# One step of a two-layer diffusion backbone: modulation in units of 1024 columns, and the low one-hot rows by VectorE

## The chip, the core and the metric

The kernel runs on one core of a Trainium2 chip. The core has TensorE (PE), which multiplies matrices, VectorE (DVE), ScalarE (ACT), GpSimd (POOL) and SyncE (SP). SP issues nearly all DMA transfers, in the order of the program; POOL issues the indirect gathers. Work on one engine runs in program order, and the engines wait for each other by semaphores. The metric is the device time of one execution in microseconds.

## The reference

Two layers run over 384 tokens, 128 of a prompt and 256 of a sample. Cut to what matters here:

```python
def adaln(cond, w, b):
    m = jax.nn.silu(cond) @ w + b
    return jnp.split(m[..., None, :], 6, axis=-1)

def layer(x, l, cond, ctx):
    sh1, sc1, g1, sh2, sc2, g2 = adaln(cond, w_mod[l], b_mod[l])
    y, new_ctx = token_mixer(modulate(x, sh1, sc1), w_in[l], ...)
    x = layer_norm(DN_ALPHA * x + g1 * y, ln1_g[l], ln1_b[l])
    f = peer(modulate(x, sh2, sc2), peer_wq[l], peer_keys[l], peer_u[l], peer_v[l])
    x = layer_norm(DN_ALPHA * x + g2 * f, ln2_g[l], ln2_b[l])

def peer(h, wq, keys, u_tab, v_tab):
    s = jnp.einsum('thpd,hpkd->thpk', q, keys)      # q = t @ wq
    sv, si = lax.top_k(s, PEER_TOPK)
    ...                                             # 16 experts e, gates g for each of 8 heads
    act = jax.nn.gelu(jnp.einsum('td,ted->te', tb, u_tab[eb])) * gb
    return jnp.einsum('te,ted->td', act, v_tab[eb])
```

`cond` is one vector of 1024 for the prompt and one for the sample, and `w_mod[l]` is 1024 x 6144: each layer has six modulation vectors of 1024 (shift, scale, gate for the mixer and for the experts). `token_mixer` is one projection `h @ w_in`, a state-space scan, two attentions, three branch projections and `w_out`.

## The kernel before

**Weights and buffers.** Every large weight comes as a tile `w` of 128 x 1024 f32 (0.52 MB) from one pool of eight buffers (`N_RAW`): `w_in` blocks, `w_mod` tiles, `peer_wq` blocks, the chunks `peer_uT` and `peer_v`, and also the staging tiles of the gate table. A load is issued by SP (L210, L1148) when its buffer's last reader is done. A projection block is cast by ACT (L222, `uh`), its rest is taken by DVE or POOL (L224, `ul`), and PE runs 24 matmuls for it (L368 to L370).

**Modulation.** The work is 48 units (layer, vector, half of 512 columns by quarters). `adaln_unit` loads two tiles (`load_k`), runs eight matmuls of `condT` (L259, which the trace shows as sixteen records) over four column groups of the PE array, ACT copies the sums to `modp` (L261), and, when the next unit is begun or at a flush, two matmuls with a selection (L265) turn them into columns, to which ACT adds the bias into `mcol` (L268). The function `adaln(n, ...)` begins n units and finishes those begun earlier. It is called in five places: in layer 0's start, two units before every second `k`, each flushed, and then the ACT rows `hraw` (L444) that need them; in `blocks`, which hands out projection blocks, one unit after each second block until `N_FILL` (16 in layer 0, 8 in layer 1) are used; after the mixer's branches, `N_AD` (4 each, as far as there are units); and in `tick` in layer 0's retrieval, one unit a block from block 6 on.

**Experts.** `finding` (the retrieval) runs over 16 `wq` blocks: queries (L947), keys, transposes, and on DVE the top-16 search. The first 35 chunks of `u` (`LAG` - 1) are multiplied whole (`u_product`, L1164, sixteen records a chunk): 14 or 18 of them behind the retrieval, the others in the gate stage; each step first loads the chunk of the next step.

**Gate stage.** `gate_table` writes, for each of 256 sample tokens, a 128 x 128 table of gates to DRAM (`gd`), as a product of one-hot rows. In each of 16 batches of 16 tokens DVE makes `oa` (L997), `ol` (L999) and `ohh` = `ol` x `ghT` (L1001), all 128 x 2048 f16, in two buffers each; sixteen ACT instructions scale `ol` by `glT` in place (L1004); PE multiplies `oa` with `ohh` and `ol` (L1014, L1015), 32 matmuls; four ACT copies go to two `w` tiles (L1018), which SP writes to `gd` (L1021). `slot` hangs two gathers of `peer_u` rows (L1057) and their dot products on DVE (L1062) behind an instruction of the batch; the dot products of the prompt's tokens run in this way beside all that.

**Order.** Within a stage a scheduler orders the instructions of each engine by due times; `tc.issue_after` and `slot` pin some of them. The order of SP is the program's: a load that waits for a buffer holds back all that is queued behind it.

Of the kernel before, what the change touches and what calls it, by code (L numbers as in the profile page):

```python
# [155 lines left out]
def hybrid_step(ctx: ExitStack, tc: tile.TileContext, A, O):  # L156
# [71 lines left out]
    fill_ps, fill_n, first = [None], [0], [0]  # L228


    def cond_prep(sp, ps1):
# [12 lines left out]
        for l in range(DEPTH):
            bm = mk(sp, [48, 128], "bm", bufs=2)
            dma(out=bm, in_=A["b_mod"][l].rearrange("(k p) -> k p", p=128))
            ps = mk(ps1, [128, 512], "pt")
            T.transpose(ps[:, :48], bm, ident[:48, :48])
            V.tensor_copy(bmT[:, l], ps[:, :48])
            for part in (1, 4):  # L250
                V.tensor_scalar(bmT[:, l, part * KD:(part + 1) * KD], bmT[:, l, part * KD:(part + 1) * KD], 1.0, None, op0=ALU.add)
# [166 lines left out]
    def mixer(l, stack, right, ps1):  # L418
# [940 lines left out]
```

## Time and profile before

| | us |
|---|---|
| median of 3 runs (lowest, highest) | 2998.48 (2995.82, 3007.12) |
| the profiled execution | 3004.09 |
| its span in the trace | 3002.3 |
| PE busy | 2855.6 (95%) |
| DVE busy | 2309.1 (77%) |
| ACT busy | 1396.8 (47%) |
| POOL busy | 824.8 (27%) |

The stages follow one another: layer 0 has its mixer to about 560 us, retrieval to about 717, gate stage to about 862 and then the main loop over the 128 chunks; layer 1 the same from about 1540, with the retrieval from 2046, the gate stage from 2195 to 2326. Busy shares are means over stages with different limits, so a window or a chain is read for each. A chain names, for each stretch of time, the engine that was working or the transfer that was landing when everything behind it waited. A matmul on f32 data shows as two records. Engine time that others wait for is on the path; idle time of an engine that isn't on the path costs nothing.

### The profile page before, as it was taken

The numbers are of one execution on the slowest core, as the hardware profiler recorded it, in microseconds if no ns is written. First come the engines' busy times: TensorE is split into PE (matmuls) and PEld (weight loads), VectorE is DVE, ScalarE is ACT, GpSimd is POOL, SyncE is SP. The second block draws the span as 40 slices with busy tenths as digits, with TensorE's granted clock in tenths as the row PEclk, the third lists the DMA queues.
The fourth block names the chain that finished last, engine by engine and source line by source line (L and its number), as shares of the span: only waits on it lengthen the run. The fifth ranks groups of instructions, "written<-read, shape, count | busy, mean of one in ns | idle before, by whom it ended". The sixth has DMA issues, their size and how long they took to land.

```text
span 3002.3 us, 48719 instructions
## 1 busy us (share of the span) xinstructions
PE 2855.6 (95%) x17953; PEld 2479.3 (83%) x17953; DVE 2309.1 (77%) x4888; ACT 1396.8 (47%) x2861; POOL 824.8 (27%) x566
## 2 busy tenths in 40 slices
PE   7999999999889999999969999999987999999996
PEld 5888889877779999998858888898876999999985
DVE  3645654599669999998976466547986999999988
ACT  4544543225754444444445455432178544444443
POOL 1000000002334455554540000000033444555554
PEclk9999999999889999999979999999999999999998
DMA  6454322565999999999934432233569999999994
GB/s 246 151 159 146 95 72 87 182 223 167 316 364 408 391 392 396 393 391 369 379 97 144 127 93 74 85 111 113 156 217 371 418 395 392 394 391 394 393 364 166
DMA packets 299328, 767.09 MB, mean 256 GB/s; under 512 B 42770, under 2 KB 113874, under 8 KB 299090
## 3 DMA queue, kind: packets, MB, share of 16 engines
q1 hardware_dynamic: 225362, 495.51, 46.2%
q0 software_dynamic: 73728, 268.47, 23.5%
q8 instruction: 141, 2.31, 0.3%
q14 instruction: 97, 0.79, 0.1%
HBM read 726.92 MB, written 36.96 MB: 254 GB/s over the span
## 4 chain that ended last, share of the span: by engine, by line
PE 74%; DVE 11%; DMA 6%; ACT 4%; issue 4%; POOL 1%; SPq 0%; POOLq 0%; ACTq 0%; DVEq 0%
PE hp L1167 6%; PE out L1243 6%; PE hp L1169 6%; PE out L1245 6%; PE hp L1168 6%; PE out L1244 6%; PE pp L368 5%; PE pp L369 5%; PE pp L370 5%; PE hp L1164 4%; DMA w<-in_peer_uT 3%; PE pp L947 2%; ACT ol L1004 2%; DVE vl L224 2%; DVE tn L1073 2%
## 5 line engine op out<-in xcount | busy, mean ns | idle before, releaser
L1057 POOL DMA_INDIRECT prow<-in_peer_u,ei x256 | 363.1, 1418 | 763.1 <-DVE prow L1062 523.5
L1068 POOL DMA_INDIRECT prow<-in_peer_v,ei x256 | 382.4, 1494 | 350.1 <-DVE tn L1073 308.6
L222 ACT CAST vh<-w 128x1024 fp32r<-128x1024 f32 x256 | 268.9, 1050 | 367.9 <-issue 285.8
L1167 PE MATMUL hp<-hh,uh 128*128 128x256 f32 x1488 | 434.7, 292 | 0.0
L1169 PE MATMUL hp<-hh,ul 128*128 128x256 f32 x1488 | 417.1, 280 | 0.0
L1168 PE MATMUL hp<-hl,uh 128*128 128x256 f32 x1488 | 416.5, 280 | 0.0
L1245 PE MATMUL out<-vh,al 128*128 128x512 f32 x1024 | 400.0, 393 | 3.6 <-DVE al L1230 3.6
L1244 PE MATMUL out<-vl,ah 128*128 128x512 f32 x1024 | 397.5, 390 | 2.9 <-DVE vl L224 2.9
L1243 PE MATMUL out<-vh,ah 128*128 128x512 f32 x1024 | 392.9, 400 | 1.4 <-ACT ah L1228 1.4
L224 DVE TENSOR_TENSOR vl<-w,vh 128x1024 fp32r<-128x1024 f32 x256 | 315.8, 1234 | 62.7 <-ACT vh L222 44.0
L1073 DVE SCALAR_TENSOR_TENSOR tn<-prow,pact,tn 128x1024 f32<-128x1024 f32 x254 | 325.4, 1281 | 2.7
L1155 ACT CAST uh<-w 128x1024 fp32r<-128x1024 f32 x186 | 195.2, 1050 | 252.6 <-PE hp L1168 240.6
L368 PE MATMUL pp<-hh,uh 128*128 128x384 f32 (+1 forms) x848 | 297.9, 351 | 7.5 <-ACT hh L344 3.8
L1062 DVE SCALAR_TENSOR_TENSOR prow<-prow,tn 128x1024 f32<-128x1024 f32 x256 | 302.4, 1219 | 0.1
L1164 PE MATMUL hp<-hs,w 128*128 128x256 f32 x1120 | 270.1, 398 | 30.0 <-DMA w<-in_peer_uT 30.0
L370 PE MATMUL pp<-hh,ul 128*128 128x384 f32 (+1 forms) x848 | 297.0, 350 | 1.4 <-POOL ul L224 1.4
L369 PE MATMUL pp<-hl,uh 128*128 128x384 f32 (+1 forms) x848 | 294.8, 348 | 0.2 <-DVE xr L494 0.2
L1167 PEld LDWEIGHTS hp<-hh,uh 128*128 128x128 f32 x1488 | 281.1, 189 | 0.0
L1169 PEld LDWEIGHTS hp<-hh,ul 128*128 128x128 f32 x1488 | 281.1, 189 | 0.0
L1168 PEld LDWEIGHTS hp<-hl,uh 128*128 128x128 f32 x1488 | 281.1, 189 | 0.0
L224 DVE TENSOR_TENSOR ul<-w,uh 128x1024 fp32r<-128x1024 f32 x124 | 149.8, 1208 | 162.2 <-ACT uh L222 158.2
L1164 PEld LDWEIGHTS hp<-hs,w 128*128 128x128 f32 x1120 | 218.8, 200 | 63.4 <-DMA w<-in_peer_uT 33.1
(401 smaller groups left out, 5637.9 us busy)
## 6 DMA issues: line engine op xcount, KB each, us to landing
w<-in_peer_uT SPq DMA_DIRECT2D x256, 512.0 KB
w<-in_peer_v SPq DMA_DIRECT2D x256, 512.0 KB
w<-in_w_in SPq DMA_DIRECT2D x104, 512.0 KB
w<-in_w_mod SPq DMA_DIRECT2D x96, 512.0 KB
gd<-w SPq DMA_DIRECT2D x64, 512.0 KB
gt<-gd SPq DMA_DIRECT2D x64, 512.0 KB
w<-in_peer_wq SPq DMA_DIRECT2D x32, 512.0 KB
w<-in_w_branch SPq DMA_DIRECT2D x24, 512.0 KB
```

Of the source, the lines that this page charges most:

```text
L224: e.tensor_tensor(lo, src, hi.bitcast(F32), op=ALU.subtract)
L368: T.matmul(o, wh[:, k, :], hh[:, k, :], start=(k == 0), stop=False)
L369: T.matmul(o, wh[:, k, :], hl[:, k, :], start=False, stop=False)
L370: T.matmul(o, wl[:, k, :], hh[:, k, :], start=False, stop=(k == KD - 1))
L1073: V.scalar_tensor_tensor(acc, row, act[:, j:j + 1], acc, op0=ALU.mult, op1=ALU.add)
L1164: T.matmul(o, ut[0][:, k, :], hs[:, k, :], start=(k == 0), stop=(k == KD - 1))
L1167: T.matmul(o, uh[:, k, :], hh[:, k, :], start=(k == 0), stop=False)
L1168: T.matmul(o, uh[:, k, :], hl[:, k, :], start=False, stop=False)
L1169: T.matmul(o, ul[:, k, :], hh[:, k, :], start=False, stop=(k == KD - 1))
L1243: T.matmul(o, ah[:, ts], vh[:, ns], start=f, stop=False)
L1244: T.matmul(o, ah[:, ts], vl[:, ns], start=False, stop=False)
L1245: T.matmul(o, al[:, ts], vh[:, ns], start=False, stop=e)
```

## The change

**Modulation** is made in 12 units of 1024 columns instead of 48. `UNITS` lists them; the first two hold four k of shift and of scale of layer 0 each, the others one vector. A unit loads eight tiles (the host lays `w_mod` out that way), and each tile is used by four matmuls of 256 columns (32 in a unit, as many in all as before). ACT copies once, two transposes of 128 x 128 replace the selections, and two DVE additions (four in the first two units) take the bias and write `mcol`. The host also lays out `b_mod` and the conditions, so their transposes at the start go. At the start one unit runs before k = 0 and one before k = 4. `blocks` begins one after every sixth block (`FILL_BY`), five in layer 0 and at most two in layer 1, where one is left; one stands behind the branches of layer 0; `tick` begins one at blocks 9, 12 and 15 of layer 0's retrieval.

**The low one-hot rows** are made by one DVE instruction a batch, `ol` x `glT`, with `glT` now f16. `slot` hangs on it instead of on `ohh`.

**Chunks ahead of the main loop** are loaded three steps ahead (`U_AHEAD`), the first three before the retrieval loop.

```diff
-N_FILL = (16, 8)
-N_AD = (4, 4)
+N_FILL = (5, 2)
+FILL_BY = 6
+N_AD = (1, 1)
+U_AHEAD = 3
-R_AD = 4
+UNITS = [((0, 0, 0, 4), (0, 1, 0, 4)), ((0, 0, 4, 4), (0, 1, 4, 4))]
+UNITS += [((l, part, 0, 8),) for l, part in ((0, 2), (0, 3), (0, 4), (1, 0), (1, 1), (0, 5), (1, 2), (1, 3), (1, 4), (1, 5))]
...
-    def adaln_unit(l, part, hb, ps1, tags):
+    def adaln_unit(u, ps1, tags):
 
-        w = load_k(A["w_mod"][l, part * 4 + hb])
         ps = mk(ps1, [128, 512], tags[0])
         for k in range(KD):
-            q = k % 4
-            T.matmul(ps[32 * q:32 * q + 32, :256], condT[:, k, :], w[k], start=(k < 4), stop=(k >= 4), tile_position=(0, 32 * q))
+            w = mk(wst, [128, RAWC], "w")
+            dma(out=w, in_=A["w_mod"][u, k])
+            for q in range(4):
+                T.matmul(ps[32 * q:32 * q + 32, :256], condT[:, k, :], w[:, q * 256:(q + 1) * 256], start=(k == 0), stop=(k == KD - 1), tile_position=(0, 32 * q))
         mp = mk(outer, [128, 256], "modp", bufs=2)
         S.copy(mp, ps[:, :256])
         yield
         pt = mk(ps1, [128, 512], tags[1])
         for a in range(2):
-            T.matmul(pt[:, 2 * a:2 * a + 2], mp[:, a * 128:(a + 1) * 128], sel, start=True, stop=True)
-        c = part * KD + 2 * hb
-        for a in range(2):
-            S.activation(mcol[:, l, part, 2 * hb + a, :], pt[:, 2 * a:2 * a + 2], AF.Identity, bias=bmT[:, l, c + a:c + a + 1])
+            T.transpose(pt[:, a * 128:(a + 1) * 128], mp[:, a * 128:(a + 1) * 128], ident)
+        pv = pt[:, :256].rearrange("p (a q m) -> p q a m", a=2, q=4)
+        j = 0
+        for l, part, k0, n in UNITS[u]:
+            for c in range(2):
+                V.tensor_tensor(mcol[:, l, part, k0:k0 + n, c].rearrange("p (q a) -> p q a", a=2), pv[:, j // 2:(j + n) // 2, :, c],
+                                bmT[:, l, part * KD + k0:part * KD + k0 + n].rearrange("p (q a) -> p q a", a=2), op=ALU.add)
+            j += n
...
-            if j % 2 and fill_n[0] > 0:
+            fill_at[0] += 1
+            if fill_n[0] > 0 and fill_at[0] % FILL_BY == 0:
...
-                    if k % 2 == 0:
-                        adaln(2, ps1, ("pp", "pt"), True)
+                    if k % 4 == 0:
+                        adaln(1, ps1, ("pp", "pt"), True)
...
-        glT = mk(rp, [128, NS], "glT")
+        glT = mk(rp, [128, NS], "glT", dt=F16)
...
-                slot(V.tensor_tensor(oh, ol, bc(ghT), op=ALU.mult))
-                for r in range(TB):
-                    o = ol[:, r // 2, :, r % 2]
-                    S.activation(o, o, AF.Copy, scale=glT[:, b * TB + r:b * TB + r + 1])
+                V.tensor_tensor(oh, ol, bc(ghT), op=ALU.mult)
+                slot(V.tensor_tensor(ol, ol, bc(glT), op=ALU.mult))
...
-        u_load(0)
+        for c in range(U_AHEAD):
+            u_load(c)
 
         def u_step(i):
-            if i + 1 < LAG - 1:
-                u_load(i + 1)
+            if i + U_AHEAD < LAG - 1:
+                u_load(i + U_AHEAD)
             u_product(i)
...
-            if l == 0 and b >= N_WQ + R_AD:
+            if l == 0 and b in (9, 12, 15):
                 adaln(1, pu, ("uT", "hp"), b == 15)
```

**SP in the mixer.** Ahead of layer 0's neighbourhood attention SP issues, before, two tiles of a unit (`in_w_mod`) after each two blocks of `in_w_in` (`ck` and `cv` are cached keys and values):

```order
L210 DMA w_1892<-in_w_mod 128x1024
L210 DMA w_1894<-in_w_mod 128x1024
L210 DMA w_1912<-in_w_in 128x1024
L210 DMA w_1950<-in_w_in 128x1024
L210 DMA w_1988<-in_w_mod 128x1024
L210 DMA w_1990<-in_w_mod 128x1024
L724 DMA ck_2322<-in_cache_na_k 128x512
L726 DMA cv_2324<-in_cache_na_v 128x512
L210 DMA w_2017<-in_w_in 128x1024
L210 DMA w_2057<-in_w_in 128x1024
```

and now (the last five of a unit's eight loads, then the first of six blocks):

```order
L255 DMA w_1709<-in_w_mod 128x1024
L255 DMA w_1715<-in_w_mod 128x1024
L255 DMA w_1721<-in_w_mod 128x1024
L255 DMA w_1727<-in_w_mod 128x1024
L255 DMA w_1733<-in_w_mod 128x1024
L726 DMA ck_2208<-in_cache_na_k 128x512
L728 DMA cv_2210<-in_cache_na_v 128x512
L214 DMA w_1746<-in_w_in 128x1024
L214 DMA w_1784<-in_w_in 128x1024
```

Eight loads for one unit stand in a row, and the block behind them is the ninth user of eight buffers.

**SP in layer 0's retrieval.** Before, two tiles of a unit and one block of `in_peer_wq` take turns:

```order
L210 DMA w_6254<-in_w_mod 128x1024
L210 DMA w_6256<-in_w_mod 128x1024
L210 DMA w_6274<-in_peer_wq 128x1024
L210 DMA w_6319<-in_w_mod 128x1024
L210 DMA w_6321<-in_w_mod 128x1024
L210 DMA w_6339<-in_peer_wq 128x1024
```

Now three blocks stand between two units (the end of one unit, three blocks, the beginning of the next):

```order
L255 DMA w_5846<-in_w_mod 128x1024
L255 DMA w_5852<-in_w_mod 128x1024
L255 DMA w_5858<-in_w_mod 128x1024
L255 DMA w_5864<-in_w_mod 128x1024
L214 DMA w_5872<-in_peer_wq 128x1024
L214 DMA w_5917<-in_peer_wq 128x1024
L214 DMA w_5962<-in_peer_wq 128x1024
L255 DMA w_6008<-in_w_mod 128x1024
```

A block of `wq` again stands behind eight loads, while `w` buffers also hold the first three chunks of `u`.

**DVE in layer 0's gate stage.** A batch before, and the beginning of the next (`oa`, `ol`, `ohh` as above, L1062 the dot products of the gathered rows `prow`):

```order
L997 TENSOR_TENSOR oa_7010<-iot_6854,i1T_6850 128x2048
L999 TENSOR_TENSOR ol_7012<-iot_6854,i2T_6851 128x2048
L1001 TENSOR_TENSOR ohh_7014<-ol_7012,ghT_6852 128x2048
L1062 SCALAR_TENSOR_TENSOR prow_7016,hd_6888<-prow_7016,tn_4726 128x1024
L1062 SCALAR_TENSOR_TENSOR prow_7019,hd_6888<-prow_7019,tn_4726 128x1024
L997 TENSOR_TENSOR oa_7095<-iot_6854,i1T_6850 128x2048
L999 TENSOR_TENSOR ol_7097<-iot_6854,i2T_6851 128x2048
L1001 TENSOR_TENSOR ohh_7099<-ol_7097,ghT_6852 128x2048
```

and two batches now (L1004 is the new instruction, line numbers of the changed kernel):

```order
L999 TENSOR_TENSOR oa_6900<-iot_6704,i1T_6700 128x2048
L1004 TENSOR_TENSOR ol_6832<-ol_6832,glT_6703 128x2048
L1062 SCALAR_TENSOR_TENSOR prow_6837,hd_6739<-prow_6837,tn_4628 128x1024
L1062 SCALAR_TENSOR_TENSOR prow_6840,hd_6739<-prow_6840,tn_4628 128x1024
L1001 TENSOR_TENSOR ol_6902<-iot_6704,i2T_6701 128x2048
L999 TENSOR_TENSOR oa_6983<-iot_6704,i1T_6700 128x2048
L1003 TENSOR_TENSOR ohh_6904<-ol_6902,ghT_6702 128x2048
L1001 TENSOR_TENSOR ol_6985<-iot_6704,i2T_6701 128x2048
L1004 TENSOR_TENSOR ol_6902<-ol_6902,glT_6703 128x2048
L1062 SCALAR_TENSOR_TENSOR prow_6907,hd_6739<-prow_6907,tn_4628 128x1024
L1062 SCALAR_TENSOR_TENSOR prow_6910,hd_6739<-prow_6910,tn_4628 128x1024
L1003 TENSOR_TENSOR ohh_6987<-ol_6985,ghT_6702 128x2048
```

A batch has six instructions instead of five, and the new one comes after a part of the next batch's rows: `oa` and `ol` of a later batch stand between `ohh` and the scaled `ol` of an earlier one.

## Rows read from the trace of the kernel before

**Rows 1.** The page, the chain that ended last: share of the span by engine
```profile
PE 74%; DVE 11%; DMA 6%; ACT 4%; issue 4%; POOL 1%; SPq 0%; POOLq 0%; ACTq 0%; DVEq 0%
```

**Rows 2.** Windows: us, busy us of each engine (instructions), PE clock, DMA share, GB/s
```profile
75.00:490.00 415.00, 410.20 (x2635) 351.37 (x2635) 230.51 (x505) 193.47 (x452) 0.00 (x0) 0.98 0.41 127
2094.00:2197.00 103.00, 101.89 (x533) 90.19 (x532) 102.00 (x594) 18.93 (x43) 4.74 (x5) 1.00 0.42 128
770.00:862.00 92.00, 72.87 (x528) 62.62 (x526) 49.07 (x61) 67.38 (x201) 28.76 (x18) 0.89 0.95 309
2197.00:2326.00 129.00, 99.75 (x784) 84.84 (x783) 94.20 (x114) 112.91 (x339) 50.20 (x32) 0.93 0.99 335
```

**Rows 3.** Timeline of the start: start us, us, engine, line, operation, releaser
```profile
38.05 1.26 ACT L444 ACTIVATE hraw<-pa,mcol 128x128 f32<-128x128 f32 x3
...
46.22 1.26 ACT L444 ACTIVATE hraw<-pa,mcol 128x128 f32<-128x128 f32 x3
49.33 0.69 PE L368 MATMUL pp<-hh,uh 128*128 128x384 f32 x1 [3.52 <-ACT uh L222]
```

**Rows 4.** Windows of the start, the fourth of 5 us
```profile
15.00:20.00 5.00, 4.68 (x30) 2.34 (x26) 1.02 (x4) 2.12 (x5) 0.00 (x0) 1.00 1.03 420
```

**Rows 5.** Timeline of PE, a fill of layer 0's mixer
```profile
194.97 1.07 PE L259 MATMUL pp<-w,condT 128*32 128x256 f32 x16
195.97 0.61 PE L265 MATMUL pt<-cst,modp 128*128 128x2 f32 x4
196.50 0.49 PE L752 MATMUL pa<-nk,nq 64*128 64x128 f32 x4
```

**Rows 6.** The chain of the whole run in time: start us, us, what
```profile
9.71 3.85 DMA w<-in_w_mod
...
567.59 3.46 PE pp L947 x16
573.72 3.46 PE pp L947 x16
...
602.12 3.46 PE pp L947 x16
610.41 3.46 PE pp L947 x16
...
746.21 10.01 DMA w<-in_peer_uT
```

**Rows 7.** The page, costliest groups: line, operation, count, busy us, mean ns
```profile
L222 ACT CAST vh<-w 128x1024 fp32r<-128x1024 f32 x256 | 268.9, 1050 | 367.9 <-issue 285.8
```

**Rows 8.** Groups of layer 0's gate stage, 719 to 860 us
```profile
L1004 ACT ACTIVATE ol<-ol,glT 128x128 f16<-128x128 f16 x256 | 77.7, 437 | 0.3 <-DVE ohh L1001 0.2
L1057 POOL DMA_INDIRECT prow<-in_peer_u,ei x32 | 53.0, 1657 | 136.9 <-DVE prow L1062 132.0 <-issue 4.9
L1001 DVE TENSOR_TENSOR ohh<-ol,ghT 128x2048 f16<-128x2048 f16 x16 | 19.6, 1224 | 0.5
```

**Rows 9.** Line 947 in either layer: ns min/median/max, first and last start us
```profile
L947 PE MATMUL pp<-hs,w x224: 379/379/382, 561.3 to 663.2; 128*128 128x256 f32 x112
...
L947 PE MATMUL pp<-hs,w x224: 379/379/382, 2046.4 to 2129.3; 128*128 128x256 f32 x112
```

**Rows 10.** Line 997 in either layer
```profile
L997 DVE TENSOR_TENSOR oa<-iot,i1T x16: 1218/1221/1226, 716.6 to 843.4; 128x2048 f16<-128x2048 f16 x16
...
L997 DVE TENSOR_TENSOR oa<-iot,i1T x16: 1218/1225/1226, 2194.8 to 2299.6; 128x2048 f16<-128x2048 f16 x16
```

**Rows 11.** Chains by line, 719 to 870 us, then 2194 to 2330 us
```profile
by line: DMA w<-in_peer_uT 31.2%; PE hp L1164 28.4%; ACT ol L1004 17.0%; ACT w L1018 6.0%; DMA gd<-w 3.8%; DMA gt<-gd 3.0%; issue 2.6%; PE pn L1015 1.1%; PE pn L1014 0.9%; DVE ohh L1001 0.8%; PE pp L1014 0.8%; PE pp L1015 0.8%; DVE ol L999 
...
by line: DMA w<-in_peer_uT 27.9%; ACT ol L1004 26.8%; PE hp L1164 14.2%; ACT w L1018 10.1%; DMA gd<-w 4.7%; issue 3.2%; DMA gt<-gd 3.1%; SPq L1021 1.5%; DVE ohh L1001 0.9%; ACT gel L1171 0.9%; PE hp L1167 0.9%; DVE oa L997 0.8%; PE hp L1168
```

**Rows 12.** Timeline of DVE at the end of layer 1's gate stage
```profile
2299.57 1.23 DVE L997 TENSOR_TENSOR oa<-iot,i1T 128x2048 f16<-128x2048 f16 x1 [1.21 <-PE pp L1015]
2300.71 1.22 DVE L999 TENSOR_TENSOR ol<-iot,i2T 128x2048 f16<-128x2048 f16 x1
```

More of the change, by code (lines that the diff above doesn't have):

```diff
@@ L227, in hybrid_step @@
     spool = [None]
-    fill_ps, fill_n, first = [None], [0], [0]
+    fill_ps, fill_n, fill_at, first = [None], [0], [0], [0]
     def cond_prep(sp, ps1):
-        cond = mk(sp, [16, 128], "cond")
-        dma(out=cond[0:8, :], in_=A["c_ctx"].rearrange("(k p) -> k p", p=128))
-        dma(out=cond[8:16, :], in_=A["c"].rearrange("o (k p) -> (o k) p", p=128))
+        cond = mk(sp, [128, 16], "cond")
+        dma(out=cond, in_=A["cond"])
+        dma(out=bmT, in_=A["b_mod"])
         V.memset(condT, 0.0)
-        ps = mk(ps1, [128, 512], "pt")
-        T.transpose(ps[:, :16], cond, ident[:16, :16])
@@ L238, in cond_prep @@
         th = mk(sp, [128, 16], "cth")
-        S.activation(th, ps[:, :16], AF.Tanh, scale=0.5)
+        S.activation(th, cond, AF.Tanh, scale=0.5)
         cc = mk(sp, [128, 16], "cc")
-        S.activation(cc, ps[:, :16], AF.Copy, scale=0.5)
+        S.activation(cc, cond, AF.Copy, scale=0.5)
         V.scalar_tensor_tensor(condT[:, :, 0:2].rearrange("p k c -> p c k"), th.rearrange("p (c k) -> p c k", c=2), 1.0,
                                cc.rearrange("p (c k) -> p c k", c=2), op0=ALU.add, op1=ALU.mult)
[L244 to L251, printed above, removed]
@@ L253, in adaln_unit @@
-    def adaln_unit(l, part, hb, ps1, tags):
-        w = load_k(A["w_mod"][l, part * 4 + hb])
+        for part in (1, 4):
+            b = bmT[:, :, part * KD:(part + 1) * KD]
+            V.tensor_scalar(b, b, 1.0, None, op0=ALU.add)
+    def adaln_unit(u, ps1, tags):
         ps = mk(ps1, [128, 512], tags[0])
         for k in range(KD):
-            q = k % 4
-            T.matmul(ps[32 * q:32 * q + 32, :256], condT[:, k, :], w[k], start=(k < 4), stop=(k >= 4), tile_position=(0, 32 * q))
+            w = mk(wst, [128, RAWC], "w")
+            dma(out=w, in_=A["w_mod"][u, k])
+            for q in range(4):
+                T.matmul(ps[32 * q:32 * q + 32, :256], condT[:, k, :], w[:, q * 256:(q + 1) * 256], start=(k == 0), stop=(k == KD - 1), tile_position=(0, 32 * q))
@@ L264, in adaln_unit @@
         for a in range(2):
-            T.matmul(pt[:, 2 * a:2 * a + 2], mp[:, a * 128:(a + 1) * 128], sel, start=True, stop=True)
-        c = part * KD + 2 * hb
-        for a in range(2):
-            S.activation(mcol[:, l, part, 2 * hb + a, :], pt[:, 2 * a:2 * a + 2], AF.Identity, bias=bmT[:, l, c + a:c + a + 1])
-    todo = []
-    for l, ps in ((0, (0, 1)), (0, (2,)), (0, (3, 4)), (1, (0, 1)), (0, (5,)), (1, (2,)), (1, (3, 4)), (1, (5,))):
-        todo += [(l, part, hb) for hb in range(4) for part in ps]
+            T.transpose(pt[:, a * 128:(a + 1) * 128], mp[:, a * 128:(a + 1) * 128], ident)
[6 more added lines that the diff above has]
+            j += n
+    todo = list(range(len(UNITS)))
     begun = []
@@ L449, in mixer @@
                 ln_mod_T(l, t, 0, 1, sp, mk(sp, [128, D], "xn", bufs=3), ps1, "pt", raw, lambda ks: parts(raw[:, ks], hh[:, ks, ts], hl[:, ks, ts], V if t == 2 else G))
-        fill_ps[0], fill_n[0], first[0] = ps1, N_FILL[l], N_FIRST
+        fill_ps[0], fill_n[0], fill_at[0], first[0] = ps1, N_FILL[l], 0, N_FIRST
         ysT = [mk(mo, [128, 4, NTOK], f"y{i}", dt=F32 if i else F32R) for i in range(3)]
@@ L1329, in blocked @@
     d["peer_wq"] = cut(d["peer_wq"], KD, 128)[:, :, 0]
-    d["w_mod"] = cut(d["w_mod"], 4, 256)
+    m = d["w_mod"].reshape(DEPTH, KD, 128, 6, KD, 128)
+    d["w_mod"] = np.stack([np.concatenate([m[l, :, :, part, k0:k0 + n].reshape(KD, 128, n * 128) for l, part, k0, n in u], axis=2) for u in UNITS])
+    d["b_mod"] = d["b_mod"].reshape(DEPTH, 48, 128).transpose(2, 0, 1)
+    d["cond"] = np.concatenate([d.pop("c_ctx").reshape(KD, 128), d.pop("c").reshape(KD, 128)]).T
     d["w_out"] = cut(d["w_out"], 4, 256)
```

2 lines of the change are left out of this document (1 added, 1 removed).

## The prediction

> **What bounds the kernel now.** I read the chain of the whole run first, then the windows of its stages, then the rows inside each stage that the change touches. By the chain [rows 1], TensorE (PE) sets 74% of the time, VectorE (DVE) 11%, DMA 6%, ScalarE (ACT) 4%. The windows [rows 2] split that: in layer 0's mixer PE is busy 410 of 415 us; in layer 1's retrieval DVE is busy 102.0 of 103 us; in the gate stages (770 to 862 us and 2197 to 2326 us) no engine is full, ACT has the most work in layer 1's (112.9 of 129 us), and the DMA share is 0.95 and 0.99. So each part of the change has another price in each stage.
>
> **Start, gain 10 (5 to 15).** The modulation of the first two vectors is made in turns: two k at a time go through matmuls, ACT copy, PE selections and ACT columns to the rows `hraw`, and only then comes the next turn. From one `hraw` at 38.05 to the next at 46.22 [rows 3] a turn takes 8.17 us. It needs four loads of 0.52 MB, 2.1 MB, which at the 420 GB/s of 15 to 20 us [rows 4] is 5.0 us; so the turns, not the loads, set the pace, and the first projection matmul starts at 49.33 [rows 3]. Afterwards the same bytes are two units of eight loads with one such chain behind each. The first load lands at 9.71 + 3.85 = 13.6 [rows 6]; fifteen more at 0.52 MB / 420 GB/s = 1.25 us end at 32.3. Behind the last one stand copy, transposes and DVE adds, for which I take 2 us (an estimate: less than the 3.1 us of `hraw`, cast and split below), and the `hraw` rounds of four k: from 46.22 to 49.33 two k took 3.1 us [rows 3], so 6.2. That makes 40.5 against 49.33, and a little more, since projections on the first four k can already run: 10. With loads at 350 GB/s it is 5, with the projections fully overlapped 15.
>
> **Mixer of layer 0, loss 2 (-10 to +4).** PE is full there, so PE time counts in full. An old unit costs 194.97 to 196.50, 1.53 us [rows 5]; sixteen are 24.5. A new unit has four times the matmuls, 4 x 1.00 (194.97 to 195.97) = 4.0, and two 128x128 transposes for the selections, 0.53 as these; five of 4.5 are 22.5, so 2 are saved. Against that stands a new wait: a unit fills all eight `w` buffers, and the `w_in` load behind it (the order of SP in the mixer) can start only when the unit's first matmuls free a buffer. It lands 3.85 us later [rows 6], and its cast takes 1.05 [rows 7], its split about as much: 6.1 us, against 4.5 us of unit, so PE stands for 1.6 us if projections follow at once, and not at all where scan or attention work follows. I take 0.8 for each of five, 4. Worst: 2.5 each; best: none, and somewhat quicker matmuls.
>
> **Units after the branches and in layer 1, gain 2 and 8.** After its branches layer 0 has one new unit (4.5) where four old ones were (6.1): 2 (0 to 3). Layer 1 had eight fills and two more, 15.3 us at 1.53; it keeps one unit, 4.5, with perhaps 1.6 of wait: 8 (2 to 10).
>
> **Retrieval of layer 0, loss 1 (-8 to +6).** A block without a unit takes 573.72 - 567.59 = 6.13 us, one with a unit 610.41 - 602.12 = 8.29 [rows 6]; ten units are 21.6 us of PE. They become three. Yet the stage can gain little: from its first `wq` matmul to its first `oa` it takes 716.6 - 561.3 = 155.3 us, and in layer 1, without units, 2194.8 - 2046.4 = 148.4 [rows 9, 10], because there DVE is the bound [rows 2]. So 6.9 is the most. Against it, the three chunks loaded ahead hold three of eight buffers through this stage; a unit's last three loads wait for a buffer, and the `wq` load behind waits for the unit's matmuls (the order of SP in the retrieval). One landing of 3.85 inside the unit and a little of one behind it: 4.5 + 5 us a unit, 28 for three, 7 more than now on PE, part of it under DVE's work. I take -1.
>
> **Gate stage of layer 0, gain 15 (3 to 25).** This is the largest term. A batch is (843.4 - 716.6) / 15 = 8.45 us between its first and last `oa` [rows 10]. In its chain DMA of `uT` chunks has 31.2%, PE on `hp` 28.4%, ACT on `ol` 17.0% [rows 11]: sixteen activations a batch, 77.7 us in 16 batches, 4.86 each [rows 8], then PE, then ACT `w`, then SP, with the next `uT` load queued on SP behind the writes of `w`; such a load was waited for 10.01 us [rows 6]. Both links are cut: ACT's 4.86 becomes one DVE instruction, and a chunk is asked for three steps ahead, about two batches or 14 us. What is late next? DVE: four one-hot instructions and two dot products, which start 1.14 us apart (2299.57 to 2300.71, [rows 12]), 6 x 1.14 = 6.9 us. The added one has not been seen; I price it by L1001 (1224 ns [rows 8]), which has the same form, 128x2048 f16 with two tensors in. The DMA engines: layer 1's gate moves 335 GB/s x 129 us = 43 MB [rows 2], 2.7 MB a batch, in 6.99 us a batch ((2299.6 - 2194.8) / 15, [rows 10]); at 335 GB/s flat a batch is 8.0. PE was busy 99.75 us of those 129 [rows 2] and has room. So 6.9 to 8.0; I take 7.3, since layer 1's row is nearest, with 17 `u` products in its batches where layer 0 has 21: 1.15 x 16 = 18, less 3 for DVE waiting on PE before `oa`, when both `oa` buffers are in use: 15. The gathers hang on the new instruction, one place later than now; POOL is busy 53.0 us of 141 [rows 8], so that is nothing.
>
> **Gate stage of layer 1, gain 2 (-10 to +10).** The same edit, another bound: 6.99 us a batch now against 6.9 of DVE. In the loop there is nothing to win. ACT's share of its chain, 26.8% [rows 11], can end as the first and the last batch's 4.86 us, up to 10 saved; if DVE goes on waiting for PE now and then, the added 16 x 1.22 = 19.6 us come half on top, 10 lost.
>
> The main loops, PE bound, keep their work: 0. **Sum:** 10 - 2 + 2 + 8 - 1 + 15 + 2 = 34 us. The profiled run took 3004.09, so 2970; it lay 5.6 over the median of 2998.48, and against that the time is 2964.5, 2965.
>
> **A rule against the new DVE instruction.** While POOL issued gathers for 53.0 us of this stage, at 1657 ns each, L1001 took its 1224 ns, as in layer 1 the pace of 1.14 us a start [rows 8, 12]. The Trainium skill (SBUF — State Buffer, section Who interferes with whom) says that a VectorE instruction with two SBUF inputs shares an interface with a GpSimd instruction that reads SBUF, and that the later one is blocked to the end of the earlier. By that rule the trace doesn't agree on DVE's side; whether the gathers are longer for it, no row here shows.
>
> **Rivals.** (A) The gate is held by what the edit doesn't move: DMA at 8 us a batch, or DVE, which with 6.9 us of work waits for PE a little in every batch. For it: DMA shares of 0.95 and 0.99 [rows 2]. Against: layer 1's 6.99 us. Layer 0 then gains 3, layer 1 loses 8: 34 - 12 - 10 = 12, 2986. Chance 0.19. That the `ol` edit does nothing because the `uT` waits take its place is part of this case. (B) More: 6.9 us a batch in layer 0 (25), the first and last batches of layer 1 (8), a start of 15: 34 + 10 + 6 + 5 = 55, 2943. Chance 0.13. (C) Slower: bursts of eight loads starve PE. A unit's loads come 1.25 us apart, 10 us for eight, where its matmuls take 4.0; if they aren't ahead, and the next block's 6.1 us comes on top, a unit loses some 10 us. Ten units (five fills, one after the branches, three in the retrieval, one in layer 1) at 5 us more than I counted are 50, 3015. It decides from 34 / 10 = 3.4 us a unit beyond my sum. Against it: in the mixer the DMA share is 0.41 [rows 2], so loads run ahead of PE. Chance 0.06. (D) DVE and the gathers exclude each other: each added instruction stands behind one gather of 1.66 us, 16 x 1.66 = 27 us a stage, 53 for both, 3018. Against it: L1001's 1224 ns. Chance 0.02. (The rule above is this case.)
>
> **Numbers.** The forecast, 2948 to 2983, has 0.60. The range, 2946 to 2990, reaches over A and towards B; C, D and the far half of B stay out. A measurement tells about 0.5%, 15 us, from no change: the border is 2983.5. Faster 0.71 (forecast and B, less 0.02 at the edge), same 0.21 (A and that edge), slower 0.08 (C and D).
>
> **What would show it.** First projection matmul near 40 us instead of 49.33. `oa` to `oa` near 7.3 us in both gate stages, DVE over 90% busy there, hardly any PE wait for `uT`. In the mixer, PE waits of 1 to 2 us for casts behind some of the five units. Layer 0's retrieval at 150 to 163 us from first `wq` matmul to first `oa`. I am wrong by A if DVE waits for PE before each `oa`, by C if PE waits behind units sum to over 20 us.

## The result, and the profile after

The changed kernel takes 2965.4 us (median of four executions), against 3002.3 us of the kernel before on the same chip; the ratio is 0.987 with an interval of 0.984 to 0.991. One of the four ran in a slow state (3453.2 us at a granted clock of 0.757) and isn't in the ratio; the median of the other three is 2961.9. The forecast was 2965. The sum came true, and four of its seven terms lay outside their bounds: the start and both mixers above, the retrieval below; so the terms are what is to be learnt from.

The profiled execution has a span of 2967.2 us, 35.1 less than before. Its chain by engine (the page), against [rows 1]:

```profile
PE 73%; DVE 14%; DMA 6%; issue 3%; ACT 1%; POOL 1%; SPq 0%; POOLq 0%; ACTq 0%; DVEq 0%
```

ACT's share fell from 4% to 1%, DVE's rose from 11% to 14%: the low one-hot rows have changed engines on the path, too.

Lines 949 and 999 are 947 and 997 of before (first `wq` matmul and `oa`), in layer 0, then in layer 1. They answer to [rows 9, 10]; the columns are the same.

```profile
L949 PE MATMUL pp<-hs,w x224: 379/379/421, 538.5 to 645.4; 128*128 128x256 f32 x112
...
L949 PE MATMUL pp<-hs,w x224: 379/379/382, 2006.6 to 2089.5; 128*128 128x256 f32 x112
...
L999 DVE TENSOR_TENSOR oa<-iot,i1T x16: 1211/1216/1225, 708.0 to 819.0; 128x2048 f16<-128x2048 f16 x16
...
L999 DVE TENSOR_TENSOR oa<-iot,i1T x16: 1211/1217/1226, 2155.0 to 2264.4; 128x2048 f16<-128x2048 f16 x16
```

From such first and last starts, all of one profiled execution of each kernel, each stage has a length. "Gate" runs from the first `oa` to the first matmul of the main loop (L1167), "mixer" from the first to the last projection matmul, and "behind the branches" from there to the first `wq` matmul.

| stage | before, us | after, us | gained | forecast (bounds) |
|---|---|---|---|---|
| start to first projection | 49.3 | 32.6 | 16.7 | 10 (5 to 15) |
| mixer, layer 0 | 434.2 | 429.8 | 4.4 | -2 (-10 to 4) |
| behind the branches | 77.8 | 76.1 | 1.7 | 2 (0 to 3) |
| retrieval, layer 0 | 155.3 | 169.5 | -14.2 | -1 (-8 to 6) |
| gate, layer 0 | 151.0 | 137.3 | 13.7 | 15 (3 to 25) |
| main loop to layer 1's first projection | 679.9 | 679.4 | 0.5 | 0 |
| mixer and behind, layer 1 | 498.9 | 481.9 | 17.0 | 8 (2 to 10) |
| retrieval, layer 1 | 148.4 | 148.4 | 0.0 | 0 |
| gate, layer 1 | 131.6 | 135.3 | -3.7 | 2 (-10 to 10) |
| the rest | 676 | 677 | -1.0 | 0 |
| sum | | | 35.1 | 34 |

**The start.** The timeline after, against [rows 3]: the last modulation matmuls come at 30.26, when their load has landed (32.3 was forecast), and the first projection matmul only 2.3 us behind.

```profile
30.26 0.64 PE L257 MATMUL pp<-w,condT 128*32 128x256 f32 x8 [0.59 <-DMA w<-in_w_mod]
30.96 0.37 ACT L259 COPY modp<-pp 128x256 f32<-128x256 f32 x1 [4.29 <-PE pp L257]
31.39 0.44 PE L263 MATMUL pt<-cst,modp 128*128 128x128 f32 x2 [0.49 <-ACT modp L259]
31.46 1.04 ACT L226 CAST uh<-w 128x1024 fp32r<-128x1024 f32 x1
31.86 0.37 DVE L269 TENSOR_TENSOR mcol<-pt,bmT 128x4 f32<-128x4 f32 x4 [4.60 <-PE pt L263]
32.41 1.26 ACT L446 ACTIVATE hraw<-pa,mcol 128x128 f32<-128x128 f32 x3
32.56 0.69 PE L369 MATMUL pp<-hh,uh 128*128 128x384 f32 x1 [0.73 <-ACT uh L226]
```

The second unit's `hraw` begins at 32.41 and the first projection matmul at 32.56: the projections on the first four k run beside the `hraw` rounds of the other four.

**The retrieval of layer 0.** PE's timeline over one new unit, and the windows beside it (us, busy us of PE, PEld, DVE, ACT and POOL with their instructions, PE clock, DMA share, GB/s):

```profile
611.32 3.62 PE L949 MATMUL pp<-hs,w 128*128 128x256 f32 x16
614.87 1.05 PE L257 MATMUL uT<-w,condT 128*32 128x256 f32 x10
615.85 0.94 PE L923 MATMUL pn<-gel,qT 128*128 128x128 f32 x6
616.72 1.50 PE L257 MATMUL uT<-w,condT 128*32 128x256 f32 x22
618.42 0.64 PE L257 MATMUL uT<-w,condT 128*32 128x256 f32 x8 [0.21 <-DMA w<-in_w_mod]
620.65 0.64 PE L257 MATMUL uT<-w,condT 128*32 128x256 f32 x8 [1.59 <-DMA w<-in_w_mod]
621.92 0.64 PE L257 MATMUL uT<-w,condT 128*32 128x256 f32 x8 [0.63 <-DMA w<-in_w_mod]
624.50 1.08 PE L257 MATMUL uT<-w,condT 128*32 128x256 f32 x8 [1.94 <-DMA w<-in_w_mod]
626.07 0.69 PE L263 MATMUL hp<-cst,modp 128*128 128x128 f32 x2 [0.49 <-ACT modp L259]
626.55 3.51 PE L917 MATMUL pp<-prow,w 128*128 128x128 f32 x16
629.90 3.62 PE L949 MATMUL pp<-hs,w 128*128 128x256 f32 x16
```

```profile
620.00:625.00 5.00, 1.78 (x24) 0.51 (x24) 5.00 (x35) 0.00 (x0) 0.00 (x0) 0.80 0.93 345
625.00:630.00 5.00, 4.51 (x27) 3.93 (x20) 5.00 (x37) 0.37 (x1) 0.00 (x0) 0.52 0.83 329
```

The fifth to eighth tile each end a wait for a load (4.4 us in all). PE, busy 1.78 of 5 us at 0.80, then runs at a granted clock of 0.52, which is its lower level, through 625 to 630 us; sixteen key matmuls (L917) take 3.51 us there and 2.05 at full clock. From one block to the next it is 18.6 us (611.32 to 629.90) where a block without a unit takes 6.13 [rows 6]: 12.4 us for this unit. Its loads arrive late because of SP's queue:

```profile
591.96 26.24 SPq L255 DMA_DIRECT2D w<-in_w_mod  x8
618.29 3.38 SPq L214 DMA_DIRECT2D w<-in_peer_wq  x3
```

Its eight issues spread over 26.2 us, each after a buffer is free; the last comes at 618.2, when four of its tiles are already multiplied. Over the three units PE's waits for such loads (us in total, times, longest; 535 to 720 us) are:

```profile
PE uT L257 <- DMA w<-in_w_mod: 11.0, 11, 1.9
```

### The profile page after: what moved, and what is told of

Read it like the earlier page. It is cut to its first block, busy times and chain, and to the rows that moved or that the text cites. A ratio compares the mean times of both kernels' runs of the same rounds, so it can differ in the third digit from the quotient of the medians.

```text
span 2967.2 us, 47730 instructions
## 1 busy us (share of the span) xinstructions
PE 2805.7 (95%) x17782; PEld 2445.8 (82%) x17782; DVE 2351.3 (79%) x4944; ACT 1228.7 (41%) x2217; POOL 822.6 (28%) x566
## 4 chain that ended last, share of the span: by engine, by line
PE 73%; DVE 14%; DMA 6%; issue 3%; ACT 1%; POOL 1%; SPq 0%; POOLq 0%; ACTq 0%; DVEq 0%
PE hp L1167 6%; PE out L1244 6%; PE out L1246 6%; PE hp L1169 6%; PE hp L1168 6%; PE out L1245 6%; PE pp L371 4%; PE pp L369 4%; PE pp L370 4%; PE hp L1164 3%; DMA w<-in_peer_uT 3%; PE pp L949 2%; DVE vl L228 2%; DVE tn L1073 2%; PE hp L1225 1%
## 5 line engine op out<-in xcount | busy, mean ns | idle before, releaser
L1167 PE MATMUL hp<-hh,uh 128*128 128x256 f32 x1488 | 434.8, 292 | 0.0
L1062 DVE SCALAR_TENSOR_TENSOR prow<-prow,tn 128x1024 f32<-128x1024 f32 x256 | 302.3, 1218 | 0.8 <-DMA prow<-in_peer_u,ei 0.8
L1167 PEld LDWEIGHTS hp<-hh,uh 128*128 128x128 f32 x1488 | 281.2, 189 | 0.0
L1164 PEld LDWEIGHTS hp<-hs,w 128*128 128x128 f32 x1120 | 211.3, 194 | 57.7 <-DMA w<-in_peer_uT 31.1
L352 POOL TENSOR_TENSOR res<-res,lg 128x384 f32<-128x384 f32 x6 | 8.8, 1464 | 894.7 <-ACT res L314 894.7
```

Of the source, the lines that this page charges most:

```text
L1164: T.matmul(o, ut[0][:, k, :], hs[:, k, :], start=(k == 0), stop=(k == KD - 1))
L1167: T.matmul(o, uh[:, k, :], hh[:, k, :], start=(k == 0), stop=False)
```

## The experiments

All ratios are to the kernel before on the same chip; the bracket is the interval. Stage lengths are taken as in the table above, "batch" is the first to the last `oa` over 15. Each length comes from one profiled execution; in layer 0 kernels with the same instructions in the gate stage differ by up to 0.23 us a batch.

| kernel | ratio | retrieval 0, us | batch 0 / 1, us | mixer 1, us |
|---|---|---|---|---|
| before | 1 | 155.3 | 8.45 / 6.99 | 424.7 |
| changed | 0.987 (0.984 to 0.991) | 169.5 | 7.40 / 7.29 | 407.2 |
| one chunk ahead | 0.988 (0.985 to 0.991) | 155.1 | 7.49 / 7.17 | 411.6 |
| old modulation | 0.996 (0.994 to 0.998) | 155.3 | 7.49 / 7.15 | 418.0 |
| old `ol` (ACT) | 0.986 (0.983 to 0.989) | 168.9 | 7.02 / 6.70 | 412.2 |
| no units in the retrieval | 0.987 (0.985 to 0.990) | 147.0 | 7.41 / 7.23 | 417.1 |
| chunks behind the retrieval | 0.988 (0.986 to 0.990) | 163.3 | 7.38 / 7.36 | 408.5 |
| units in four pieces | 0.984 (0.982 to 0.987) | 156.8 | 7.33 / 7.21 | 407.3 |
| half of `ol` on ACT | 0.990 (0.988 to 0.993) | 169.3 | 6.99 / 7.62 | 411.7 |

**One chunk ahead.**

```diff
-U_AHEAD = 3
+U_AHEAD = 1
```

> The changed kernel with the chunks loaded one ahead again. Layer 0's retrieval takes 169.5 us from its first wq matmul (L949) to its first oa, 14 more than before. Theory (burst): a unit's eight loads stand in a row behind too few free buffers, PE waits for them and its clock falls; seven free buffers instead of five are still too few, so the stage stays within 5 us of 169.5. Rival (chunks): the three chunks that hold buffers through the stage cause it, and it falls to 158 or less. Gate stage of layer 0, now 7.4 us a batch: 8.2 or more if loading ahead did the work there, 7.4 to 7.6 if the DVE instruction alone did. Total: burst and loading ahead 2975, chunks 2955, neither 2965.

The retrieval came back to 155.1 us, so by this pair the three chunks and their buffers cause the 14 us, and I had expected the burst. In the gate stage the batch stayed at 7.49: with the DVE instruction in place, loading ahead is worth 0.09 us a batch there, less than kernels differ in any case (the whole stage took 141.0 us instead of 137.3). Against the 14.4 us of the retrieval stand some 13 us lost elsewhere, the most of them in this stage, in layer 1's mixer (4.4) and behind layer 0's branches (3.1), and the total is that of the changed kernel.

**Old modulation.** The kernel before with the two other parts of the change.

```diff
-        glT = mk(rp, [128, NS], "glT")
+        glT = mk(rp, [128, NS], "glT", dt=F16)
...
-                slot(V.tensor_tensor(oh, ol, bc(ghT), op=ALU.mult))
-                for r in range(TB):
-                    o = ol[:, r // 2, :, r % 2]
-                    S.activation(o, o, AF.Copy, scale=glT[:, b * TB + r:b * TB + r + 1])
+                V.tensor_tensor(oh, ol, bc(ghT), op=ALU.mult)
+                slot(V.tensor_tensor(ol, ol, bc(glT), op=ALU.mult))
...
-        u_load(0)
+        for c in range(U_AHEAD):
+            u_load(c)
...
-            if i + 1 < LAG - 1:
-                u_load(i + 1)
+            if i + U_AHEAD < LAG - 1:
+                u_load(i + U_AHEAD)
```

> The kernel before with the DVE instruction for ol and the chunks three ahead, that is the changed kernel with the old modulation. Start: first projection matmul back at 49 us (32.6 now). Layer 1's mixer, now 407 us from first to last projection matmul against 425 before: theory (unit work only, 8 x 1.53 less one new unit) says 415 and no more, since the rest was a granted clock that fell in other places by chance; rival (the small units bring the low clock) says 425 again with stretches at 0.5 to 0.9. Retrieval 155 if the bursts of new units cost the 14 us. Gate of layer 0 stays near 7.4 us a batch. Total 2985 to 2995.

The retrieval is 155.3 us with three chunks held and the old units. So chunks alone cost nothing more, and new units alone (one chunk ahead) cost nothing more: it takes both, a run of eight loads and five free buffers. The start is back at 46.8. Layer 1's mixer is between the two forecasts, 418.0; the clock is treated with the terms below. By this kernel's ratio of 0.996 the two other parts are worth 0.4% and the new modulation 0.9%, with its loss in the retrieval and whatever the clock did.

**Old `ol`.**

```diff
-        glT = mk(rp, [128, NS], "glT", dt=F16)
+        glT = mk(rp, [128, NS], "glT")
...
-                V.tensor_tensor(oh, ol, bc(ghT), op=ALU.mult)
-                slot(V.tensor_tensor(ol, ol, bc(glT), op=ALU.mult))
+                slot(V.tensor_tensor(oh, ol, bc(ghT), op=ALU.mult))
+                for r in range(TB):
+                    o = ol[:, r // 2, :, r % 2]
+                    S.activation(o, o, AF.Copy, scale=glT[:, b * TB + r:b * TB + r + 1])
```

> The changed kernel with ol made by 16 ScalarE activations a batch again. Theory: in layer 0's gate the batch goes from 7.4 us to 8.0 or more (ACT's chain is back), in layer 1's from 7.29 back to 6.99. Rival: loading ahead made the gain in layer 0, which then stays at 7.6 or less. Total: theory 2965 + 10 - 5 = 2970, rival 2962.

Layer 0's batch is 7.02 us, the shortest so far: the rival, and beyond it. With the chunks three ahead, ACT makes the rows faster than DVE does, in both layers. The first `oa` rows of the kernel:

```profile
L999 DVE TENSOR_TENSOR oa<-iot,i1T x16: 1218/1226/1284, 707.0 to 812.3; 128x2048 f16<-128x2048 f16 x16
...
L999 DVE TENSOR_TENSOR oa<-iot,i1T x16: 1218/1225/1300, 2153.5 to 2254.0; 128x2048 f16<-128x2048 f16 x16
```

**No units in the retrieval.** Layer 1's mixer gets two more instead, and the third stands behind its branches.

```diff
-N_FILL = (5, 2)
+N_FILL = (5, 3)
...
-            if l == 0 and b in (9, 12, 15):
-                adaln(1, pu, ("uT", "hp"), b == 15)
```

> The changed kernel without units in layer 0's retrieval; one more unit in layer 1's mixer, the two others there too (three fills), the last behind its branches. Burst theory: retrieval 169.5 down to 148 to 150, as layer 1's; mixer of layer 1 up by 5 to 6 a unit, three units for one; total 2965 - 20 + 13 = 2958. Rival (a unit costs the same wherever PE is busy): no change, 2965.

As the burst theory had it: the retrieval takes 147.0 us, like layer 1's, although three chunks are held. Layer 1's mixer paid 9.9 us for two units in this profile (6.6 of it work, by the table further down) and the stretch behind its branches 3.8 for one. A unit costs less there than the 12.4 us in the retrieval; in the mixer the loads run ahead of PE.

**Chunks behind the retrieval.** The three first loads move behind the loop over the blocks.

```diff
-        for c in range(U_AHEAD):
-            u_load(c)
...
         next(finding)
+        for c in range(U_AHEAD):
+            u_load(c)
         u_steps(N_EXP[l])
```

> The changed kernel with the three first chunks loaded behind the retrieval loop instead of ahead of it; units and everything else as changed. With one chunk held the retrieval took 155.1 us, with three and the old units 155.3, with three and the new units 169.5 and 168.9. Theory (eight loads need the buffers that the chunks hold): 155 or less here, gate stage as changed (7.4 us a batch), total 2965 - 14 = 2951. Rival (it is when the chunks are asked for later, not the buffers): retrieval 165 or more, 2963.

Neither number came. The `wq` blocks got faster as the theory says (first to last 92.7 us, 106.9 in the changed kernel), the stage only to 163.3. PE stood before the eighth chunk product:

```profile
660.91 3.72 PE L1164 MATMUL hp<-hs,w 128*128 128x256 f32 x16 [0.47 <-ACT gel L1171]
673.29 25.95 PE L1164 MATMUL hp<-hs,w 128*128 128x256 f32 x112 [8.65 <-issue]
```

**Units in four pieces.** The retrieval's units with two tiles a block, from block 4 on; three chunks held.

```diff
-    def adaln_unit(u, ps1, tags):
+    def adaln_unit(u, ps1, tags, step=0):
...
+            if step and k and k % step == 0:
+                yield
             w = mk(wst, [128, RAWC], "w")
...
-            if l == 0 and b in (9, 12, 15):
-                adaln(1, pu, ("uT", "hp"), b == 15)
+            if l == 0 and b >= 4:
+                if b % 4 == 0:
+                    parted.append(adaln_unit(todo.pop(0), pu, ("uT", "hp"), 2))
+                next(parted[-1])
+                if len(parted) > 1:
+                    next(parted.pop(0), None)
+                if b == 15:
+                    next(parted.pop(0), None)
```

> The changed kernel with the three units of the retrieval taken in four pieces of two tiles, one piece a block from block 4 on; the chunks still hold three buffers. Theory (the burst of eight against five free buffers): PE no longer waits for w_mod, retrieval 155 or less, total 2951. Rival (fewer buffers make every load late): the wq blocks wait too, retrieval 162 or more, 2960.

156.8 us, 12.7 less than in a burst with the same bytes and the same five buffers, and PE no longer waits for `w_mod`: nearly all of the loss was the burst. A little stays (155 was forecast; the total is 2956.5 us for 2951). The pieces also begin at block 4 instead of 9, and this run doesn't tell that from the cut.

**Half of `ol` on ACT.** ACT scales eight rows of a batch, DVE the others in one instruction of half the size.

> The changed kernel with eight of a batch's sixteen rows scaled by ScalarE and eight by one VectorE instruction of half the size. DVE then has 6.3 us a batch and ACT some 4.7. If the engines set the pace (DVE 6.9 as changed, ACT 6.8 with all sixteen): below 6.7 us a batch in both layers, total 2951 or less. If the DMA engines do (share 0.99 to 1.04 in every form so far): 6.9 to 7.1 in layer 0, 6.6 to 6.8 in layer 1, total 2956 as with ScalarE alone.

Layer 0 has 6.99 us, as the forecast for the DMA engines said, and from 710 to 800 us neither ACT nor DVE is full (the second row; the first is the old `ol`, the third the changed kernel, the fourth the first combination below, which also has `ol` on ACT):

```profile
710.00:800.00 90.00, 80.33 (x646) 69.76 (x645) 74.37 (x90) 87.73 (x270) 40.32 (x26) 1.00 1.00 342
...
710.00:800.00 90.00, 84.49 (x649) 71.18 (x648) 83.10 (x107) 61.51 (x168) 40.10 (x26) 0.98 1.00 342
...
710.00:800.00 90.00, 84.58 (x657) 72.69 (x656) 85.11 (x101) 31.33 (x65) 42.09 (x24) 0.98 0.98 332
...
710.00:800.00 90.00, 82.87 (x657) 71.95 (x655) 75.05 (x91) 88.29 (x272) 41.41 (x26) 0.98 1.05 364
```

That the old `ol` ends at the same 7.0 us doesn't show that transfers hold both. With the old `ol` ACT is busy 87.73 of 90 us, so ACT may be what holds it, and 342 GB/s is no ceiling: the fourth row has 364 at 6.95 us a batch. With half of `ol` on ACT the longest wait of ACT is for the writes of the gate table (707 to 812 us):

```profile
ACT w L1024 <- DMA gd<-w: 13.7, 6, 6.1
```

So transfers have a part in its 6.99 us; how much of it they set is not shown. Layer 1 went to 7.62, outside both forecasts, and the total to 2974.2 us (2951 or 2956 was forecast). Between 2160 and 2260 us PE waited 18.1 us for chunks there, hardly more than the 16.7 us with the old `ol` at 6.70 a batch, and DVE 22.1 us for PE, against 11.8; why is open.

**Without the chunk loads of the gate stage.**

```diff
+            if N_PRE[l] + U_AHEAD <= c < LAG - 1:
+                utp[c] = kept[0]
+                return
...
-                utp[c] = (t.rearrange("p (k e) -> p k e", k=KD),)
+                utp[c] = kept[0] = (t.rearrange("p (k e) -> p k e", k=KD),)
```

> The changed kernel without the loads of chunks 17 to 34 in layer 0 (21 to 34 in layer 1): their products use the last chunk loaded, so these columns of the expert activations are left wrong. A measurement of what sets the gate stage, now 7.40 us a batch in layer 0 and 7.29 in layer 1. If DVE's six instructions set it (6 x 1.145 = 6.9) with some waits for chunks: 6.9 to 7.0 in both. If DMA alone sets it: far below 7.4 is impossible for DVE, so it also ends at 6.9, but with a DMA share well under 0.9. If PE and DVE waiting for each other set it: 7.2 to 7.4 as now.

In this one execution (2943.0 us) the batch is 6.63 us in both layers, and DVE is full:

```profile
710.00:800.00 90.00, 89.12 (x700) 75.51 (x699) 90.00 (x106) 33.76 (x70) 47.50 (x26) 1.00 0.97 291
...
L999 DVE TENSOR_TENSOR oa<-iot,i1T x16: 1217/1226/1230, 704.6 to 804.1; 128x2048 f16<-128x2048 f16 x16
```

So DVE's six instructions and their overlap are worth 6.63 us, 0.3 below my 6.9, and the chunk loads 0.77 us a batch in layer 0 and 0.66 in layer 1, 12 and 11 us a stage. Whether by coming late or by their traffic, this run doesn't tell. My forecast for the DMA share, "well under 0.9", was wrong: it is 0.97 at 291 GB/s, and yet between 707 and 812 us neither PE nor DVE nor ACT waits for a transfer.

**PSUM tile of the unit.** The kernel with the chunks behind the retrieval, and:

```diff
-                adaln(1, pu, ("uT", "hp"), b == 15)
+                adaln(1, pu, ("uT", "uT"), b == 15)
```

> The kernel with the chunks loaded behind the retrieval loop, and the transposes of a retrieval unit in the PSUM tile uT, not in one of the three hp tiles that the chunk products use. With hp the retrieval took 163.3 us although its wq blocks took 92.7 instead of 106.9: PE stood 8.65 us before the eighth product. Theory: the hp tile was held until DVE, busy with the top-16 search, came to the unit's additions; then the stage takes 148 to 152 and the total is 2951 or less. Rival (products wait for their chunks, loaded late): 160 or more, 2964.

161.4 us instead of 163.3 (ratio 0.987, 0.984 to 0.989): the time forecast failed, and the wait has only moved to another PE instruction. There it shows its cause, which the "issue" above did not (waits of PE, 628 to 699 us: us in total, times, longest):

```profile
PE uT L263 <- DVE mcol L269: 9.0, 1, 9.0
```

PE waits until DVE has added the bias of the last unit but one, and DVE works through its top-16 search first. Before the change ACT did these additions; no run gives them back to ACT, so that this would spare the wait is not shown.

**Two combinations.** Chunks behind the retrieval with the old `ol`:

> The changed kernel with the chunks loaded behind the retrieval loop and ol made by ScalarE again. If the two effects are separate places they add: retrieval 155, layer 0's batch 7.0 and layer 1's 6.7, total 2957 - 14 = 2943. If the later chunks cost the gate stage its lead, 2950 or more.

Ratio 0.982 (0.980 to 0.985): retrieval 163.2, batches 6.95 and 6.81. The gate gains add, the retrieval has the wait just shown, and the total is 2948.6 us for 2943. With the unit's PSUM tile changed as well:

> The same with ol made by ScalarE: if both add, retrieval 150, batches 6.95 and 6.8, total 2937; if not, 2948 as without the PSUM change.

Ratio 0.984 (0.981 to 0.987), retrieval 160.8, batches 7.15 and 6.81, 2954.6 us: no better, and neither forecast. And three chunks ahead, no units in the retrieval, old `ol`:

> The changed kernel without units in layer 0's retrieval (three fills in layer 1's mixer), ol made by ScalarE, chunks three ahead. The two parts lie in different stages: retrieval 147, batches 7.0 and 6.7, total 2958 - 6 - 10 = 2942.

Ratio 0.982 (0.979 to 0.985), 2948.8 us against 2997.3: retrieval 147.0, batches 7.18 and 6.73, mixer of layer 1 422.3. The median missed 2942 by 7, as much as that mixer is longer than in the other run with three fills (417.1) plus the 0.16 us a batch. This one and the first combination are the fastest kernels of the study that do all of the work, by about half a per cent against the changed kernel; their intervals and its interval touch. Units in four pieces together with the old `ol` were not run.

## Why the prediction was right, and where it wasn't

**The start: mis-sized, 16.7 for 10.** The last load came some 2 us before the forecast, and the chain behind it took the 2 us that it was priced at. The 6.2 us of `hraw` for four k were put on the path, and I gave back only "a little" for the projections on the other four; all of it is hidden.

**Mixers: PE work right, waits too large, clock not priced.** Net of what PE waits and of what a granted clock below 1 costs (both summed over windows of 5 us between the first and last projection matmul; a window at clock c is charged 5 us times 1 - c, whether PE is busy in it or not), the mixers compare like this:

| | layer 0: net, wait, clock (us) | layer 1: net, wait, clock (us) |
|---|---|---|
| before | 419.4, 6.3, 8.5 | 403.4, 7.5, 13.8 |
| old modulation | 416.1, 6.4, 10.8 | 404.9, 8.0, 5.1 |
| changed | 413.2, 8.1, 8.5 | 395.3, 5.5, 6.5 |
| one chunk ahead | 413.0, 8.9, 8.6 | 394.4, 6.8, 10.4 |
| no units in the retrieval | 413.6, 7.9, 5.1 | 401.9, 7.0, 8.2 |

In layer 1 the net work fell by 8.1, which is the forecast of 8. The other 9 are wait (2.0) and clock (7.3). The clock is no gain of the change: with the same old units it costs 13.8 in one kernel and 5.1 in the other, with the same new unit 6.5 and 10.4. In the kernel before it is 0.84 and 0.76 in the two stretches of 10 us from 1550, at the layer's first projections (PE busy 7.10 and 9.86 us), and 0.50 from 1640 to 1650, behind a stretch of 5 us in which PE was busy only 2.94. Why it falls in one kernel and not in the other is open. In layer 0 the wait that I priced at 4 is 1.8 (8.1 less 6.3), and the work saved is 6.2 or, against the old modulation, 2.9, where 2 was forecast (the kernel before and the one with the old modulation have the same instructions there and are 3.3 apart, so no more can be read from it); a new unit costs (401.9 - 395.3) / 2 = 3.3 us of PE in layer 1, not 4.5.

**Retrieval: the step that failed.** The prediction had the right place ("a unit's last three loads wait for a buffer") and put 9.5 us on a unit, 28 for three, against 21.6 removed, and then let most of the difference vanish "under DVE's work". Both sizes were wrong. The unit shown took 12.4 us, and two units lengthened the blocks by 24.0 (first to last `wq` matmul 106.9 us, 82.9 without units), so some 36 for three: the waits for loads are 4.4 us of the one shown, and the clock that fell behind them costs PE about 2.5 more (1.78 us of work at 0.80, 4.51 at 0.52), a link that I didn't see. And DVE covers no more of it than before. The ten old units, 21.6 us, made the stage 8.3 us longer than the 147.0 it takes without units, so some 13 us of PE time were hidden already; 36 less 13 is 23, and the stage went from 147.0 to 169.5. DVE is full in the windows above, but at the stage's end it waits for PE: the index transposes stand behind fourteen chunk products in PE's order, and the wait of DVE for them (0.3 us without units, 4.0 before) was 9.1 in the changed kernel:

```profile
DVE i L976 <- PE pp L981: 9.1, 1, 9.1
```

What PE loses beyond those 13 us therefore arrives whole at the first `oa`. Layer 1's stage, from which I took the bound of 6.9, has no such wait, though its window in [rows 2] has PE at 101.89 of 103 us beside DVE's 102.00, and I named only DVE; the experiment without units (147.0) shows that the bound itself was right.

**Gate of layer 0: right in size, wrong in how it adds.** 7.40 us a batch for 7.3. I added two cures, "both links are cut", and the runs show each to be enough: 7.49 with DVE alone (one chunk ahead), 7.02 with the chunks alone (old `ol`), 7.40 with both. The DVE instruction takes the path over from ACT, and with the chunks ahead it is a loss: by four pairs of kernels that differ in `ol` alone, 0.2 to 0.4 us a batch in layer 0 (7.34 to 7.41 us by DVE, 6.95 to 7.18 by ACT) and 0.5 to 0.6 in layer 1. The four cells of that square come from four kernels, the first with the old modulation (which moves the batch by 0.09 and 0.14 where all else is equal):

| | one chunk ahead | three ahead |
|---|---|---|
| `ol` by ACT | 8.45 / 6.99 | 7.02 / 6.70 |
| `ol` by DVE | 7.49 / 7.17 | 7.40 / 7.29 |

**Gate of layer 1: the sign was wrong**, within its bounds. The loop lost 0.3 us a batch, 4.6, and the 10 us hoped for at the ends came to 0.9. "In the loop there is nothing to win" is true of the DVE instruction only: with the chunks ahead and `ol` on ACT the loop won 0.3 us a batch (6.70 for 6.99). The sign "hardly any PE wait for `uT`" failed here too: from 2155 to 2262 us PE waited for chunks eight times, 14.8 us in all, and 6.7 us in layer 0 (707 to 812).

**Rivals.** (A) did not happen: layer 0 gained 13.7, not 3, and DMA doesn't hold the stage at 8; whether it holds it at 7.0 when the engines have room is not shown. (C) happened, in the retrieval only, at 2.5 to 3 us a unit beyond what I had counted; it stayed away where I looked for it first, in the mixers. (D) did not happen: L1004 runs beside the gathers, at the time of its neighbour.

```profile
L1057 POOL DMA_INDIRECT prow<-in_peer_u,ei x31 | 53.4, 1723 | 133.5 <-DVE prow L1062 128.9 <-issue 4.6
...
L1003 DVE TENSOR_TENSOR ohh<-ol,ghT 128x2048 f16<-128x2048 f16 x16 | 19.5, 1216 | 0.0
L1004 DVE TENSOR_TENSOR ol<-ol,glT 128x2048 f16<-128x2048 f16 x16 | 19.4, 1215 | 0.0
```

By the rule of the Trainium skill (SBUF — State Buffer, Who interferes with whom) the trace agrees at most on POOL's side, where a gather is 1723 ns instead of 1657; nothing waits for that.

Sum: the start and layer 1's wait and clock gave 16 us more than forecast, the mixer of layer 0 6 more, and the retrieval and layer 1's gate took 19 back. That the gain in the profile (35.1 us) fell within 2 us of the forecast is luck.

## What to carry to other kernels

Before a chain is credited with two cures, ask what each is worth when the other is in: here either one took most of the gain, and the DVE instruction, put beside the other, moved work onto an engine that had none to spare: VectorE's own 6.63 us are now the floor of the batch. A burst of loads as large as the buffer pool is cheap only where loads run far ahead of their use, and where other tiles hold some of the buffers it should be cut into pieces. "Another engine is busy all that time" hides a wait only as far as the first engine still has slack: measure how much of it the old work already used, and whether the other engine waits at the end of the stage.

## What the runs showed of the hardware

A DMA share near 1 doesn't show that transfers are the bound: the gate stage has 0.97 at 291 GB/s with a part of its loads left out and DVE full, while 1.05 at 364 GB/s was reached in the same stretch by another kernel. The clock term of layer 1's mixer, 13.8 us in one kernel and 5.1 in another with the same instructions there, goes with stages 6.7 us apart, so a stage is better compared by its work net of the clock than by its length. A wait of 4.4 us spread over one unit was followed by some 5 us of PE at its lower clock level, which cost about 2.5 us more.
